# A hybrid decoder layer on one core: 1/rms goes into the matrix that x is turned with

## The chip, the cores and the metric

The kernel runs on one core of a Trainium2 chip, in one launch. The metric is the device time of an execution in microseconds; the median of three executions of the kernel before is 969.17 us (967.22 to 969.35). The page of the profile and the trace come from one further execution, recorded by the hardware profiler.

Engines are named as the profile names them: PE is TensorE's matrix products and PEld its weight loads, DVE is VectorE, ACT is ScalarE, POOL is GpSimd, SP is the engine whose queue issues most of the DMAs.

## The reference, cut to what matters

The layer normalises x over its 1024 features, modulates it with a vector that comes from the conditioning input c, and multiplies the result by one wide input matrix. Everything behind that (a gated convolution, a chunked retention in four heads, an output projection, a residual and a last norm) is untouched by the change.

```python
mod = silu(c) @ ada_w + ada_b
shift, scale, gate = split(mod, 3)
y = x * rsqrt(mean(x * x, axis=-1) + 1e-6)        # one factor for each of the 1024 positions
u = y * norm_g * (1 + scale) + shift              # one factor and one shift for each feature
proj = u @ w_in                                   # contracts over the features
```

The product with `w_in` contracts over the features, so u has to lie with its features on the partitions, while x comes from memory with its positions there. The factor 1/rms belongs to a position, the modulation to a feature.

## The kernel before, in words

All 1024 positions are kept on chip. x is read in eight tiles `xt` of 128 positions by 1024 features (line 170). The function `norm` (lines 172 to 188) handles one tile:

- ACT squares the tile and sums the squares into `ms` (line 175); POOL adds epsilon and raises it to the power -1/2 (lines 176, 177).
- DVE multiplies the whole tile by that factor, in place (line 178).
- PE turns the tile in two groups `xp` of four 128x128 blocks, by transposes against the identity `ident_t` (line 183). Each group is one PSUM bank, and four banks take turns.
- ACT copies the first group, DVE the second, into `xs`, which holds x turned (lines 186, 188); for the last tile DVE copies both.

Around it, `mod` (lines 190 to 200) makes the shift and the factor of one block of 128 features from a 1 MB tile `aw` of the modulation matrix: DVE does two dot products against the broadcast activation (line 193), except that the shift of block 0 is eight small products of PE (`mod0p`, line 197). `make_u` (lines 202 to 206) then makes u for that block and splits it into a rounded part `uh` (ACT) and the rest `ul` (DVE), because each product with a weight is done as three products of rounded operands (lines 82, 83, 84: uh with the weight's high part, ul with the high part, uh with the weight's low part). Block 0 is done in two halves of the positions, blocks 1 to 7 whole.

The first eight output tiles (the `ps_e` and `ps_p..` sums) accumulate over the eight feature blocks, 24 products of 512 columns for each block, while `aw` and the weights of the next blocks still arrive. This is the head of the kernel. `ps_s` follows (line 367), then 21 pairs of output tiles by a seven-product scheme (lines 469 to 493) with the convolution's taps on DVE beside them, then the retention in chunks interleaved with the values and the pointwise product (lines 540 to 703), then the output projection and the last norm. For the seven-product scheme DVE and ACT make sums of quarters of u, split as `th` and `tl` (lines 317 to 326); that work also starts in the head.

The order of every engine's instructions is set when the program is built: a list scheduler with a cost model of its own takes the code's dependences and priorities and writes one fixed order for each engine. DVE, ACT, POOL, SP and PE each run theirs strictly in order and wait by semaphores. So a changed cost in one place can move instructions elsewhere in the program. The buffers of `aw` are three, so the load for block 3 waits until block 0's `aw` has been read, by DVE and by `mod0p`.

Of the kernel before, what the change touches and what calls it, by code (L numbers as in the profile page):

```python
# [7 lines left out]
F32 = mybir.dt.float32  # L8
# [4 lines left out]
P = 128  # L13
# [34 lines left out]
def hybrid_layer(ctx: ExitStack, tc: tile.TileContext, x, vec, c_row, ada_ss, ada_g, adab_g, w_e, w_s, w_p, w_v,  # L48
                 w_pw, w_out, final_g, cs, masks, kc, ident, out):
    nc = tc.nc  # L50
    SUB, ADD, MUL = ALU.subtract, ALU.add, ALU.mult
# [47 lines left out]
    ident_t = const.tile([P, P], F32, name="ident_t")  # L99
# [36 lines left out]
    hp = head_ctx.enter_context(tc.tile_pool(name="head", bufs=1))  # L136
# [8 lines left out]
    def head():  # L145
# [26 lines left out]
        def norm(t, xt_):  # L172

            ms = hp.tile([P, 1], F32, tag="ms", name=f"ms{t}", bufs=3)
            nc.scalar.activation(junk2, xt_, AF.Square, scale=D ** -0.5, accum_out=ms)
            nc.gpsimd.tensor_scalar(ms, ms, EPS, None, op0=ADD)
            nc.gpsimd.tensor_tensor(ms, ms, mhalf[:, 0:1], op=ALU.pow)
            nc.vector.tensor_scalar(xt_, xt_, ms, None, op0=MUL)
            for q in range(2):
                tp = hps.tile([P, 4, P], F32, tag=("paa", "pbb", "pcc", "pdd")[(2 * t + q) % 4], name=f"xp{t}{q}")  # L180
                for j in range(4):
                    k = 4 * q + j
                    nc.tensor.transpose(tp[:, j], xt_[:, k * P:(k + 1) * P], ident_t)
                dst = xs[:, 4 * q:4 * q + 4, t * P:(t + 1) * P]
                if q == 0 and t < 7:
                    nc.scalar.copy(dst, tp)
                else:
                    nc.vector.tensor_copy(dst, tp)
# [36 lines left out]
        for t in range(4):  # L225
            norm(t, xts[t])
        mod(0, aw)
        make_u(0, halves(0))
        for t in range(4, TT):
            norm(t, xts[t])  # L230
# [520 lines left out]
    with tc.tile_pool(name="fin", bufs=1, reuse_waits="tile") as fp, \  # L751
# [92 lines left out]
        t = TT - 1  # L844
# [98 lines left out]
```

## Time and profile before

| | |
|---|---|
| median of three executions | 969.17 us (967.22 to 969.35) |
| the profiled execution | 970.08 us, of which 968.3 us are the span from the first to the last instruction |
| PE busy | 937.2 us, 97% of the span |
| DVE busy | 745.3 us, 77% |
| ACT busy | 412.2 us, 43% |
| POOL busy | 389.8 us, 40% |
| DMA | 154.95 MB, 160 GB/s in the mean |

Busy time is the time in which an engine had an instruction in it. The ends of PE's products are modelled, and products overlap: the time that one costs in a stream is the distance from one start to the next, which is shorter than the duration that a row gives. Where the text needs it, it is worked out from a row that covers several in a stream: (length of the row less the duration of one) divided by their count less one.

### The profile page before, as it was taken

What the parts mean: (1) busy time and instruction counts of PE and PEld (TensorE: products, weight loads), DVE (VectorE), ACT (ScalarE), POOL (GpSimd) and SP (SyncE); (2) the same over time, 40 slices, a digit from 0 to 9 for tenths busy, and PEclk for the clock granted to TensorE, in tenths of its full rate; (3) what the DMA queues carried; (4) which work ended last, traced back from release to release, by engine and by line L of the source; (5) the groups of instructions that cost most, each with busy time, mean ns of one, the idle gap of its engine ahead of it and who ended that gap; (6) DMA issues with size and microseconds to landing.
All of it is one profiled execution on the core that took longest, in us unless ns stands there. A gap on an engine that the chain in (4) does not pass through costs nothing.

```text
span 968.3 us, 12531 instructions
## 1 busy us (share of the span) xinstructions
PE 937.2 (97%) x4496; PEld 784.5 (81%) x4496; DVE 745.3 (77%) x928; ACT 412.2 (43%) x676; POOL 389.8 (40%) x358
## 2 busy tenths in 40 slices
PE   7999999999999999999999899989999999999996
PEld 5788888888888888888888688877788887888886
DVE  6999989899999999999799786687875344523322
ACT  7775433433434334343430575677634333311201
POOL 3004987877887798878550111121022100000000
PEclk9999999999999999999999899989999999999998
DMA  9924242333334444443434799555775486432111
GB/s 348 331 78 133 75 144 88 118 88 104 125 121 138 133 127 132 134 141 97 154 117 163 267 332 308 179 165 200 240 290 176 157 279 221 147 106 87 65 44 44
DMA packets 84673, 154.95 MB, mean 160 GB/s; under 512 B 6657, under 2 KB 43265, under 8 KB 83330
## 3 DMA queue, kind: packets, MB, share of 16 engines
q1 hardware_dynamic: 81986, 147.07, 45.9%
q0 software_dynamic: 1040, 3.67, 1.0%
q10 hardware_dynamic: 1584, 3.41, 0.9%
q8 instruction: 35, 0.57, 0.2%
q14 instruction: 28, 0.23, 0.1%
HBM read 107.99 MB, written 46.14 MB: 159 GB/s over the span
## 4 chain that ended last, share of the span: by engine, by line
PE 78%; DVE 10%; DMA 5%; issue 3%; ACT 2%; POOL 1%; POOLq 0%; DVEq 0%; ACTq 0%
PE pa L83 7%; PE pa L84 7%; PE pa L82 7%; DVE y L271 4%; PE ps_o L83 4%; PE ps_o L84 4%; PE ps_o L82 4%; PE pb L83 4%; PE pb L82 4%; PE pb L84 4%; PE ps_pw L82 2%; PE ps_pw L84 2%; PE ps_pw L83 2%; DMA wo<-w_out 2%; PE pd L84 2%
## 5 line engine op out<-in xcount | busy, mean ns | idle before, releaser
L271 DVE SCALAR_TENSOR_TENSOR yp<-a,vec_t,yp 128x1024 f32<-128x1024 f32 x210 | 269.7, 1284 | 6.7 <-ACT yp L269 2.7
L334 POOL TENSOR_TENSOR pl<-pr,ph 128x512 fp32r<-128x512 f32 x63 | 84.7, 1345 | 59.7 <-ACT ph L333 59.5
L334 POOL TENSOR_TENSOR pl_s<-sm_s,ph_s 128x512 fp32r<-128x512 f32 x63 | 85.4, 1356 | 36.6 <-ACT ph_s L333 35.1
L333 ACT CAST ph_s<-sm_s 128x512 fp32r<-128x512 f32 x63 | 39.1, 622 | 95.8 <-PE pa L83 80.3
L333 ACT CAST ph<-pr 128x512 fp32r<-128x512 f32 x63 | 39.1, 622 | 79.7 <-PE pa L83 45.4
L806 POOL TENSOR_TENSOR fr<-fr,mhalf 128x1 f32<-128x1 f32 x7 | 3.8, 547 | 168.0 <-DVE fr L805 168.0
L691 POOL TENSOR_TENSOR rs<-mv,kc_t 128x2 f32<-128x2 f32 x16 | 6.2, 390 | 158.7 <-DVE mv L688 133.8
L82 PE MATMUL pb<-uh,ph_s 128*128 128x512 f32 x168 | 65.4, 389 | 0.0
L84 PE MATMUL pb<-uh,pl_s 128*128 128x512 f32 x168 | 65.4, 389 | 0.0
L82 PE MATMUL pa<-th,ph_s 128*128 128x512 f32 x168 | 65.4, 389 | 0.0
L83 PE MATMUL pb<-ul,ph_s 128*128 128x512 f32 x168 | 65.4, 389 | 0.0
L84 PE MATMUL pa<-th,pl_s 128*128 128x512 f32 x168 | 65.4, 389 | 0.0
L83 PE MATMUL pa<-tl,ph_s 128*128 128x512 f32 x168 | 65.4, 389 | 0.0
L346 POOL TENSOR_TENSOR sm_s<-pr,pr 128x512 f32<-128x512 f32 x42 | 57.2, 1362 | 17.3 <-DMA pr<-w_p 10.1
L83 PE MATMUL ps_pw<-zl,hi_pw 128*128 128x512 f32 x128 | 50.4, 394 | 2.2 <-DVE zl L71 2.2
L84 PE MATMUL ps_pw<-zh,lo_pw 128*128 128x512 f32 x128 | 50.6, 395 | 0.0
L82 PE MATMUL ps_pw<-zh,hi_pw 128*128 128x512 f32 x128 | 48.0, 399 | 1.9 <-ACT zh L70 1.7
L271 DVE SCALAR_TENSOR_TENSOR y<-a,vec_t,y 128x1024 f32<-128x1024 f32 x30 | 44.1, 1469 | 6.9 <-ACT y L269 6.1
L797 DVE TENSOR_TENSOR g<-ps_o,gate 128x512 f32<-128x512 f32 x14 | 9.5, 691 | 49.7 <-PE ps_o L84 49.7
L83 PE MATMUL ps_o<-wol,hi_yc 128*128 128x512 f32 x112 | 43.8, 391 | 0.1
L83 PE MATMUL ps_o<-wol,hi_yr 128*128 128x512 f32 x112 | 43.7, 393 | 0.0
L84 PE MATMUL ps_o<-woh,lo_yc 128*128 128x512 f32 x112 | 43.6, 390 | 0.0
(447 smaller groups left out, 2792.9 us busy)
## 6 DMA issues: line engine op xcount, KB each, us to landing
pr<-w_p SPq DMA_DIRECT2D x84, 256.0 KB, 2.7
aw<-ada_ss SPq DMA_DIRECT2D x8, 1024.0 KB, 8.1
d_qk<-ro SPq DMA_DIRECT2D x16, 512.0 KB, 3.3
wo<-w_out SPq DMA_DIRECT2D x16, 512.0 KB, 4.7
xt<-x SPq DMA_DIRECT2D x8, 512.0 KB, 6.9
d_sg<-o SPq DMA_DIRECT2D x16, 256.0 KB, 2.6
sg<-d_sg SPq DMA_DIRECT2D x16, 256.0 KB, 3.5
v<-d_v SPq DMA_DIRECT2D x16, 256.0 KB, 3.4
```

What stands on the lines that cost most here:

```text
L82: nc.tensor.matmul(ps, lh, rh, start=start, stop=False, skip_group_check=more)
L83: nc.tensor.matmul(ps, lh, rl, start=False, stop=False, skip_group_check=more)
L84: nc.tensor.matmul(ps, ll, rh, start=False, stop=stop, skip_group_check=more)
L271: nc.vector.scalar_tensor_tensor(acc, ap[:, j:j + S], col(V_CW, m * CW + j), acc, op0=MUL, op1=ADD)
L333: nc.scalar.copy(hi, src)
L334: nc.gpsimd.tensor_tensor(lo, src, hi.bitcast(F32), op=SUB)
L346: nc.gpsimd.tensor_tensor(out, a, b, op=op)
L691: nc.gpsimd.tensor_tensor(rs, mv[:, :, 1], kc_t[:, K_G2 + 2 * h:K_G2 + 2 * h + 2], op=MUL)
L797: nc.vector.tensor_tensor(g[:, :n], ps(), gate[:, sl], op=MUL)
L806: nc.gpsimd.tensor_tensor(r, r, mhalf[:, 0:1], op=ALU.pow)
```

## The change

DVE no longer multiplies the tile. It multiplies the 128x128 identity by the factor 1/rms instead, one factor for each partition, which gives a diagonal matrix `dgx` (three buffers). PE does not transpose the scaled tile against the identity, but multiplies the unscaled blocks as they came by the diagonal matrix, as ordinary products of fp32: block^T times diag(1/rms) is the turned and scaled block. What is added up and where it is copied to stays as it was.

```diff
@@ -175,12 +175,13 @@
             nc.scalar.activation(junk2, xt_, AF.Square, scale=D ** -0.5, accum_out=ms)
             nc.gpsimd.tensor_scalar(ms, ms, EPS, None, op0=ADD)
             nc.gpsimd.tensor_tensor(ms, ms, mhalf[:, 0:1], op=ALU.pow)
-            nc.vector.tensor_scalar(xt_, xt_, ms, None, op0=MUL)
+            dg = hp.tile([P, P], F32, tag="dg", name=f"dgx{t}", bufs=3)
+            nc.vector.tensor_scalar(dg, ident_t, ms, None, op0=MUL)
             for q in range(2):
                 tp = hps.tile([P, 4, P], F32, tag=("paa", "pbb", "pcc", "pdd")[(2 * t + q) % 4], name=f"xp{t}{q}")
                 for j in range(4):
                     k = 4 * q + j
-                    nc.tensor.transpose(tp[:, j], xt_[:, k * P:(k + 1) * P], ident_t)
+                    nc.tensor.matmul(tp[:, j], xt_[:, k * P:(k + 1) * P], dg, start=True, stop=True)
                 dst = xs[:, 4 * q:4 * q + 4, t * P:(t + 1) * P]
                 if q == 0 and t < 7:
                     nc.scalar.copy(dst, tp)
```

Every line of the program behind line 178 moves down by one. The built order changes too, in three places that matter here.

On PE, at the end of the turning of x, this stood before (`xp60` is tile 6, first group; a row with x4 is four instructions):

```order
L183 MATMUL xp60_287<-ident_t_76,xt6_92 128x128 x4
L183 MATMUL xp61_293<-ident_t_76,xt6_92 128x128 x4
L197 MATMUL mod0p_234<-cact_82,aw0_148 128x1 x8
L183 MATMUL xp70_304<-ident_t_76,xt7_93 128x128 x4
L183 MATMUL xp71_310<-ident_t_76,xt7_93 128x128 x4
L82 MATMUL ps_e00_319<-uh0_94,weh0_152 128x512
```

And this stands there now:

```order
L184 MATMUL xp60_294<-dgx6_292,xt6_92 128x128 x3
L198 MATMUL mod0p_238<-cact_82,aw0_148 128x1 x8
L184 MATMUL xp60_294<-dgx6_292,xt6_92 128x128
L184 MATMUL xp61_300<-dgx6_292,xt6_92 128x128 x4
L184 MATMUL xp70_312<-dgx7_310,xt7_93 128x128 x4
L184 MATMUL xp71_318<-dgx7_310,xt7_93 128x128 x4
L82 MATMUL ps_e00_327<-uh0_94,weh0_152 128x512
```

The eight products of `mod0p` now have 51 of the 64 blocks of x ahead of them, where they had 56.

On DVE, from the copy of the last group of x to the first `ul` of block 1, this stood before from `ul0` on:

```order
L206 TENSOR_TENSOR ul0_102<-xs_123,uh0_94 128x512
L193 SCALAR_TENSOR_TENSOR junk_132,mod1_359<-aw1_351,cbc_130 128x1024
L206 TENSOR_TENSOR ul0_102<-xs_123,uh0_94 128x512
L320 TENSOR_TENSOR xs_123<-xs_123 128x512
L166 TENSOR_TENSOR wel1_356<-wer1_353,weh1_355 128x512
L193 SCALAR_TENSOR_TENSOR junk_132,mod2_399<-aw2_391,cbc_130 128x1024 x2
L206 TENSOR_TENSOR ul1_103<-xs_123,uh1_95 128x1024
```

And this stands there now, from that copy on:

```order
L189 COPY xs_123<-xp71_318 128x4x128
L207 TENSOR_TENSOR ul0_102<-xs_123,uh0_94 128x512
L194 SCALAR_TENSOR_TENSOR junk_132,mod2_407<-aw2_399,cbc_130 128x1024
L207 TENSOR_TENSOR ul0_102<-xs_123,uh0_94 128x512
L321 TENSOR_TENSOR xs_123<-xs_123 128x512
L194 SCALAR_TENSOR_TENSOR junk_132,mod2_407<-aw2_399,cbc_130 128x1024
L207 TENSOR_TENSOR ul1_103<-xs_123,uh1_95 128x1024
```

Both dot products of block 1 and the split of its weight went ahead of the copy of the last group; behind it six instructions stand up to and with `ul1`.

On DVE, at the end of the head, between `ul` of block 6 and of block 7, this stood before:

```order
L206 TENSOR_TENSOR ul6_108<-xs_123,uh6_100 128x1024
L321 TENSOR_TENSOR xs_123<-xs_123 128x512
L166 TENSOR_TENSOR wel7_596<-wer7_593,weh7_595 128x512
L71 TENSOR_TENSOR tl2_673<-xs_123,th2_670 128x512
L322 TENSOR_TENSOR xs_123<-xs_123 128x512
L206 TENSOR_TENSOR ul7_109<-xs_123,uh7_101 128x1024
```

And this stands there now:

```order
L207 TENSOR_TENSOR ul6_108<-xs_123,uh6_100 128x1024
L322 TENSOR_TENSOR xs_123<-xs_123 128x512
L324 TENSOR_TENSOR xs_123<-xs_123 128x512
L166 TENSOR_TENSOR wel7_604<-wer7_601,weh7_603 128x512
L323 TENSOR_TENSOR xs_123<-xs_123 128x512
L71 TENSOR_TENSOR tl2_681<-xs_123,th2_678 128x512
L71 TENSOR_TENSOR tl3_682<-xs_123,th3_679 128x512
L71 TENSOR_TENSOR tl4_683<-xs_123,th4_680 128x512
L324 TENSOR_TENSOR xs_123<-xs_123 128x512
L71 TENSOR_TENSOR tl2_681<-xs_123,th2_678 128x512
L71 TENSOR_TENSOR tl3_682<-xs_123,th3_679 128x512 x2
L207 TENSOR_TENSOR ul7_109<-xs_123,uh7_101 128x1024
```

Eleven instructions now lie between the two, where there were four.

## Rows read from the trace of the kernel before

**Rows 1.** The page: busy us by engine, share of the span, instructions.

```profile
PE 937.2 (97%) x4496; PEld 784.5 (81%) x4496; DVE 745.3 (77%) x928; ACT 412.2 (43%) x676; POOL 389.8 (40%) x358
```

**Rows 2.** Stretches: from:to, length, busy of PE, PEld, DVE, ACT, POOL, granted clock, DMA.

```profile
22.50:69.00 46.50, 44.61 (x193) 35.96 (x194) 46.47 (x71) 37.23 (x55) 0.00 (x0) 1.00 0.60 208
69.00:536.00 467.00, 465.55 (x2053) 385.06 (x2051) 445.24 (x431) 178.47 (x298) 340.74 (x257) 1.00 0.39 124
536.00:780.00 244.00, 230.33 (x1334) 201.31 (x1335) 171.49 (x318) 139.85 (x233) 36.26 (x71) 0.97 0.68 234
```

**Rows 3.** Waits of PE, 23 to 69 us: total us, times, longest us.

```profile
PE ps_e L83 <- DVE ul L206: 1.3, 3, 0.7
PE ps_e L82 <- ACT uh L204: 0.7, 1, 0.7
```

**Rows 4.** Timeline, 0 to 45 us: start, length, engine, instruction, count, idle before.

```profile
7.90 0.75 DVE L178 TENSOR_SCALAR xt<-xt,ms 128x1024 f32<-128x1024 f32 x1 [0.25 <-POOL ms L177]
...
15.69 1.06 PE L183 MATMUL xp<-ident_t,xt 128*128 128x128 f32 x8 [0.66 <-DVE xt L178]
...
19.50 1.87 PEld L197 LDWEIGHTS mod0p<-cact,aw 128*128 128x128 f32 x16
...
21.89 0.33 SPq L157 DMA_DIRECT2D aw<-ada_ss  x1
...
23.14 0.73 PE L82 MATMUL ps_e<-uh,weh 128*128 128x512 f32 x2 [0.75 <-ACT uh L204]
```

**Rows 5.** Lines by form: the multiplication removed; count, busy us, mean ns, idle before.

```profile
L178 DVE TENSOR_SCALAR xt<-xt,ms 128x1024 f32<-128x1024 f32 x8 | 6.0, 750 | 0.8 <-POOL ms L177 0.7
```

**Rows 6.** Line 583, which scales the identity in the convolution's norm: min/median/max ns.

```profile
L583 DVE TENSOR_SCALAR rs_d<-ident_t,rstd x8: 273/281/286, 634.6 to 641.3; 128x128 f32<-128x128 f32 x8
```

**Rows 7.** Timeline of PE, 3 to 12 us.

```profile
3.42 3.78 PE L221 MATMUL cp<-crow,ones_t 1*128 1x512 f32 x4 [3.42 <-ACT crow L210]
8.71 3.68 PE L183 MATMUL xp<-ident_t,xt 128*128 128x128 f32 x16 [1.51 <-DVE xt L178]
```

**Rows 8.** Timeline near 639 us: four products of fp32 with a diagonal matrix, 128 columns.

```profile
638.85 1.11 PE L584 MATMUL rb<-rs_d,ones_t 128*128 128x128 f32 x8
```

**Rows 9.** The tile xp in the windows 13.2 to 13.7 and 14.2 to 14.8 us.

```profile
L183 PE MATMUL xp<-ident_t,xt x4: 421/421/422, 12.9 to 13.5; 128*128 128x128 f32 x4
...
L183 PE MATMUL xp<-ident_t,xt x8: 272/273/324, 13.9 to 14.8; 128*128 128x128 f32 x8
```

**Rows 10.** Lines by form, 0 to 80 us: ACT's instructions in the head.

```profile
L175 ACT ACTIVATE junk<-xt 128x1024 bf16<-128x1024 f32 x8 | 8.5, 1062 | 3.3 <-DMA xt<-x 3.3
...
L165 ACT CAST weh<-wer 128x512 fp32r<-128x512 f32 x8 | 4.9, 614 | 2.2 <-PE ps_pdd L83 2.2
...
L186 ACT COPY xs<-xp 128x512 f32<-128x512 f32 x7 | 4.1, 579 | 1.0 <-PE xp L183 0.9
...
L200 ACT ACTIVATE gsc<-mod,scg,vec_t 128x1 f32<-128x1 f32 x8 | 3.1, 386 | 6.4 <-DVE junk L193 6.3
...
L204 ACT ACTIVATE uh<-xs,shift,gsc 128x512 fp32r<-128x512 f32 x2 | 1.6, 814 | 0.0
```

**Rows 11.** Timelines of DVE and of PE near 62 us: ul of block 7.

```profile
61.43 0.69 DVE L322 TENSOR_TENSOR xs<-xs 128x512 f32<-128x512 f32 x1
62.03 1.22 DVE L206 TENSOR_TENSOR ul<-xs,uh 128x1024 fp32r<-128x1024 f32 x1
...
65.35 0.39 PE L83 MATMUL ps_e<-ul,weh 128*128 128x512 f32 x1
```

**Rows 12.** The chain that ended last, near 32 us: start, length, what.

```profile
31.92 0.50 PE ps_e L83
```

**Rows 13.** The page: loads of the modulation matrix, KB each, us to landing.

```profile
aw<-ada_ss SPq DMA_DIRECT2D x8, 1024.0 KB, 8.1
```

**Rows 14.** Stretches in the retention, columns as in rows 2.

```profile
543.00:550.00 7.00, 6.01 (x28) 6.04 (x29) 6.94 (x11) 5.48 (x8) 0.00 (x0) 0.51 0.87 313
...
628.50:638.50 10.00, 7.78 (x33) 7.20 (x34) 7.84 (x21) 5.42 (x12) 3.25 (x5) 0.50 0.68 232
```

## The prediction

> **What bounds the kernel now.** I read the page first, then the sums by stretch, then PE's waits, and only then the stretch that is changed. The page shows PE busy for 97% of the span [rows 1]; the sums by stretch show where the rest lies. From 69 to 536 us PE is busy for 465.55 of 467 us, so nothing of VectorE shows there, and a shift at 69 us passes through unchanged; the retention from 536 to 780 us has most of the idle time, 244.00 - 230.33 = 13.7 us [rows 2]. In the head (22.5 to 69 us) VectorE is busy without a break, 46.47 of 46.50 us [rows 2], which looks as if it were the limit, but PE's waits in that stretch are only 1.3 us for VectorE's `ul` and 0.7 us for ACT's `uh` [rows 3]. PE and VectorE are nearly level there. So what counts is when PE can start the head's products, 23.14 us before [rows 4], and how much it waits behind that.
>
> **What the change removes.** Eight multiplications of 750 ns on VectorE [rows 5], against eight of the 128x128 form, which take 281 ns where the kernel already scales its identity [rows 6]: 8 x 0.47 = 3.8 us less of VectorE. For the first tile that lies on the path: VectorE's instruction starts at 7.90 us, when POOL's factor is there [rows 4], and PE at 8.71 [rows 7]. PE can start at 8.71 - 0.47 = 8.24 us. The other seven are beside PE's work and count only if VectorE is the limit, which is weighed below.
>
> **What it adds on PE.** A transpose is one pass. A product of two fp32 operands is two: `mod0p` is eight products in the program and 16 weight loads in the trace [rows 4], and the four products of line 584's inner loop are eight records [rows 8]. In a stream at the full clock, where one takes 0.27 us from start to end [rows 9], a transpose costs (1.06 - 0.27)/7 = 0.112 us [rows 4]; a pass of line 584 costs (1.11 - 0.27)/7 = 0.12 us with a slow first one in it [rows 8], and one of `mod0p` at most 1.87/16 = 0.117 us [rows 4]. I take 0.112 for a pass too, so a block costs 0.223 us in place of 0.112. At the lower clock, in which PE begins, transposes come every (3.68 - 0.42)/15 = 0.217 us [rows 7]. Two passes of 128 columns at that clock are not shown; the nearest rows are two transposes, 0.43 us, and the 512-column passes of line 221, at most 3.78/4 = 0.95 us each, so 0.47 us for two of a quarter of the width [rows 7]. I take 0.43.
>
> When the clock rises is a choice. The transposes take 421 ns up to 13.5 us and 273 ns from about 14 us [rows 9], that is 1.2 and 2.4 GHz, after PE had transposed without a real pause since 8.71. I keep 14.0 us, since PE is as dense as before from 8.24 us on.
>
> The Trainium skill has a rule that speaks against the products altogether: its page "TensorE: Matmul & The Clock Gate", section "Terms", says that the transpose mode is four times faster for FP32. By it a block would cost 0.45 us at the full clock; line 584's row shows two passes of the usual length, so the trace does not agree, and I go by the row. As a case of its own it stands among the rivals.
>
> **The sum up to the first product of the head.** From 8.24 to 14.0 us, 5.76/0.43 = 13.4 blocks. The other 50.6 cost 50.6 x 0.223 = 11.3 us, and `mod0p` stands among them with 16 x 0.112 = 1.8 us: 14.0 + 13.1 = 27.1 us. Before, PE waited between tiles for VectorE and ACT; now it is the slowest of the chain. ACT's square and copy of a tile, 1.06 + 0.58 us [rows 10], fit into the 8 x 0.223 = 1.8 us that a tile takes PE, and VectorE's part is smaller still. What stood between the last transpose and the head, ACT's `uh` of block 0, is now early: `mod0p` has 51 blocks ahead of it, ends at 14.0 + 37.6 x 0.223 + 1.8 = 24.2 us, and ACT needs its shift (under 0.39) and one `uh` of 0.81 us [rows 10], so 25.4 us. PE runs on without a wait at 27.1 us, 4.0 us later than 23.14.
>
> **What is given back, and what is added, up to 69 us.** VectorE now does both dot products of block 1 before the last copy of x, so only six instructions lie between that copy and the end of `ul1`: by the starts one of 512 columns takes 0.60 us; one of 1024 takes 1.22, or 1.14 with the same overlap [rows 11]. The copy can start at 27.1 + 0.3 us; it, three of 512 and three of 1024 columns give 27.4 + 0.6 + 1.8 + 3.4 = 33.2 us. Before, PE took `ul1` at 31.9 us, after a wait [rows 12]. VectorE is 1.3 us later, PE 4.0: the three waits for `ul` go, 1.3 us [rows 3], and with each the slow first product, 0.50 - 0.39 = 0.11 us [rows 11, 12], in all 1.6 us. This is all that VectorE's 3.8 us can give PE here.
>
> Two waits come in their place. First, ACT has eight instructions from the end of `mod0p` (24.2 us, plus 0.3 for the last one's length) to the second half of `uh0`: 0.81 x 3 + 0.61 + 0.58 + 0.39 x 3 at most [rows 10] = 4.8 us, so 28.5 to 29.3 us with starts that overlap or not. PE, after four products of the first half at 44.61/193 = 0.23 us [rows 2], wants it at 28.0. I take 0.6 us (0 to 1.2). Second, `ul7`. It was ready at 62.03 + 1.22 = 63.25 us and used at 65.35, 2.1 us of slack [rows 11]. Seven more instructions of 0.60 us now stand ahead of it, 4.2 us, and VectorE is 1.3 us later: 68.8 us. PE wants it at 65.35 + 4.0 - 1.6 + 0.6 = 68.35. I take 0.4 us (0 to 2).
>
> The loads do not decide. The load of `aw` for block 3 was issued at 21.89 us on SP's queue [rows 4]; now it waits for `mod0p`'s reading, 24.2 us, and stands behind the load of block 2's weight there, 0.3 us. With 8.1 us to land [rows 13] it is there at 32.6 us, and VectorE first reads it behind `ul1`, at 33.2 us; PE uses what comes of it only after all of block 2, so that a later landing has that much cover still.
>
> Sum at 69 us: +4.0 - 1.6 + 0.6 + 0.4 = **+3.4 us**. Bounds: with the clock up only at 17.5 us it is 9.26/0.43 = 21.5 blocks, 42.5 x 0.223 = 9.5 and 1.8, so 28.8 us, and with both new waits at their upper ends 5.7 - 1.6 + 3.2 = +7.3; with the clock up at 11.1 us (the first rival) and no new wait 2.6 - 1.6 = +1.0.
>
> **Behind 69 us.** Up to 536 us PE has no idle time that could take the shift up [rows 2]. In the retention the built order interleaves the chunks, the values and the pointwise products differently, and 13.7 us of PE's idle time lie there. Nothing in the trace prices an order that was not run. I take 0, with a quarter of that idle time, 3.4 us, either way.
>
> The profiled execution took 970.08 us (span 968.3 and 1.8 us around it), 0.9 above the median of the runs. So the forecast is 973.5 us against that execution, and 969.2 + 3.4 = **972.6 us** against the median.
>
> **Rivals.**
>
> *The clock rises earlier.* Products of PE proper might raise it sooner than transposes did. For it: PE has only a short pause before 8.24 us. Against: the products of line 221 kept PE busy for 3.78 us from 3.42 [rows 7], and the transposes behind them still ran at the lower clock. If it rose at 11.1 us, half-way: 2.9/0.43 = 6.7 blocks before, 57.3 x 0.223 = 12.8 behind, and 1.8: 25.7 us, a shift of 2.6, and with -0.6 as above +2.0: 971.2 us. The Trainium skill, page "TensorE: Matmul & The Clock Gate", section "Part 4: PE-mode transpose", gives a reason for this one: the full clock does not engage for transposes, since they do not count as busy as products do. The trace disagrees in that nothing but transposes ran when it rose near 14 us [rows 9]. Chance 0.17.
>
> *A block costs four passes.* 0.86 us at the lower clock, 0.45 at the full one: 6.7 blocks to 14.0 us, 57.3 x 0.45 = 25.8, and 1.8: 41.6 us, a shift of 18.5; VectorE's waits would all vanish, -1.6: about 986 us. Against it stand the counts of records [rows 4, 8]. Chance 0.03.
>
> *The retention takes it back.* The idle time there falls by 2 to 4 us in the new order: 969 to 971 us, no change. Chance 0.15.
>
> *Faster.* The place is the retention: from 543 to 550 and from 628.5 to 638.5 us the granted clock is 0.5 [rows 14], with PE busy for 6.01 of 7 and 7.78 of 10 us. If the new order closes the waits that led there, these busy times fall to half, by 6.9 us, and 973.5 - 6.9 - 0.9 = 965.7 us. It decides only if both stretches go, since one alone (3 to 3.9 us) just pays for the head. Against it: nothing of the change touches what PE waits for there. Chance 0.08.
>
> *VectorE is the limit of the head*, so that its 3.8 us come straight off. For it: 46.47 of 46.50 us busy. Against: PE waits for it 1.3 us in all, so that it can give no more than that. It is in the sum.
>
> **How the numbers follow.** The forecast has 0.57, the clock 0.17, the retention as no change 0.15, faster 0.08, four passes 0.03. The time is that of the forecast. The range is 968.8 to 976.5 us: 3.4 us of the retention on either side, with the early clock and the upper ends of the two waits. A measurement of this kernel can tell about 0.2%, 1.9 us, from no change, so no change is 967.2 to 971.1 us. Half of the early clock falls in there, and with the retention's case it is 0.23: faster 0.08, no change 0.23, slower 0.57 + 0.09 + 0.03 = 0.69.
>
> **What would show it.** Right: PE's blocks of x as 128 records in place of 64, without idle time between tiles, at twice the distance; the first product of the head near 27 us with no wait; waits for `ul` below 0.5 us up to 60 us, one for `uh0` near 28 us and a small one for `ul7` near 68 us; `ps_s` about 3.4 us later than before; VectorE's multiplications at 0.28 us. Wrong: the first product of the head before 25 us (the clock, or cheaper passes) or behind 29; a wait for `aw` in the head; or the sum of PE's idle time from 536 to 780 us off 13.7 by more than 3.4 us, in which case the order there, not the change of arithmetic, sets the sign.

## The result, and the profile after

The changed kernel takes **978.64 us** in the median of four runs (975.26 to 979.43), the kernel before beside it 969.26 (967.22 to 971.46): a ratio of **1.0084** [1.0064, 1.0103], slower with an interval well clear of no change. The forecast was 972.6 us, with 976.5 as its upper end. The sign was right, the size was not: of the 9.4 us between the medians the prediction found 3.4.

The profiled execution after took 975.26 us, the shortest of the four. Read stage by stage, its own 975.26 - 970.08 = 5.2 us over the profiled execution of before do not lie where the prediction put them. The page, against [rows 1], and then the stretches, against [rows 2], with the last one new:

```profile
PE 944.0 (97%) x4560; PEld 789.3 (81%) x4560; DVE 739.8 (76%) x928; ACT 410.8 (42%) x676; POOL 388.3 (40%) x358
```

```profile
22.50:69.00 46.50, 45.21 (x214) 37.37 (x214) 46.34 (x71) 35.46 (x54) 0.00 (x0) 1.00 0.57 207
69.00:536.00 467.00, 466.79 (x2060) 386.29 (x2059) 442.54 (x431) 180.58 (x301) 339.31 (x257) 1.00 0.38 122
536.00:780.00 244.00, 231.26 (x1342) 201.13 (x1341) 170.84 (x318) 137.50 (x232) 37.77 (x71) 0.97 0.68 232
785.00:945.00 160.00, 156.41 (x677) 125.79 (x676) 60.07 (x70) 36.35 (x52) 3.29 (x6) 1.00 0.41 132
```

PE has 4560 records for 4496, the 64 second passes, and VectorE 5.5 us less of work. From 785 to 945 us PE is now busy for 156.41 of 160 us. The same stretch of the kernel before:

```profile
785.00:945.00 160.00, 159.79 (x700) 130.86 (x698) 59.98 (x71) 36.52 (x54) 3.83 (x7) 1.00 0.40 130
```

This is the output projection, of which the prediction says nothing. PE's waits in it were none and are now these (the second row; the first is the head, against [rows 3]):

```profile
PE ps_e L83 <- DVE ul L207: 1.2, 1, 1.2
...
PE ps_o L82 <- ACT woh L70: 3.3, 4, 1.3
```

The head first, in PE's timeline (start, length, count; lines behind 178 are one higher than before), to be held against [rows 4, 7]:

```profile
7.99 13.40 PE L184 MATMUL xp<-dgx,xt 128*128 128x128 f32 x102 [0.84 <-DVE dgx L179]
21.23 1.84 PE L198 MATMUL mod0p<-cact,aw 128*128 128x1 f32 x16
22.93 3.15 PE L184 MATMUL xp<-dgx,xt 128*128 128x128 f32 x26
25.83 0.71 PE L82 MATMUL ps_e<-uh,weh 128*128 128x512 f32 x2
```

The 128 passes run without a pause, and `ps_e` follows at 25.83 us, 2.7 us later than before. The clock rose earlier than forecast, as the passes of `xp` in two windows show (the 421 ns ones against the 275 ns ones, as in [rows 9]):

```profile
L184 PE MATMUL xp<-dgx,xt x5: 421/421/421, 10.3 to 11.1; 128*128 128x128 f32 x5
...
L184 PE MATMUL xp<-dgx,xt x8: 274/275/275, 11.7 to 12.5; 128*128 128x128 f32 x8
```

Where the projection loses its time stands in SP's queue. After:

```profile
764.34 0.32 SPq L734 DMA_DIRECT2D cgl<-d_cg  x1
772.93 0.32 SPq L738 DMA_DIRECT2D d_yc<-cgl  x1
773.30 1.25 SPq L760 DMA_DIRECT2D wo<-w_out  x2
```

and before:

```profile
764.67 0.32 SPq L733 DMA_DIRECT2D cgl<-d_cg  x1
765.04 0.90 SPq L759 DMA_DIRECT2D wo<-w_out  x2
765.99 0.42 SPq L770 DMA_DIRECT2D fgt<-final_g  x1
773.43 0.33 SPq L737 DMA_DIRECT2D d_yc<-cgl  x1
```

A store of `d_yc` that waits for VectorE's product until 772.9 us now stands ahead of the first two of sixteen loads of `w_out`. They are issued at 773.30 in place of 765.04 us. All sixteen pass through two buffers, so each waits for the splitting of the last but one, and the chain of what ended last runs through them:

```profile
783.81 3.45 DMA d_yc<-cgl
...
788.33 2.91 SPq L791
...
791.35 6.08 DMA wo<-w_out
797.45 1.05 ACT woh L70
798.53 1.24 DVE wol L71
799.78 4.99 DMA wo<-w_out
```

I use two measures below. The head ends with the last product of `ps_e`: 67.3 us before, 69.7 after. *Behind the head* is a kernel's median less that time of its profile: 969.2 - 67.3 = 901.9 us before, 978.6 - 69.7 = 908.9 after. Most of the loss, about 7 us, is behind the head. The median is of several executions and the head of one, so a single value is good to a microsecond or two: by the two profiled executions alone, spans less heads, it is 901.0 and 903.7 us.

### The profile page after: what moved, and what is told of

Read it like the earlier page. It is cut to its first block, busy times and chain, and to the rows that moved or that the text cites. A ratio compares the mean times of both kernels' runs of the same rounds, so it can differ in the third digit from the quotient of the medians.

```text
span 973.4 us, 12654 instructions
## 1 busy us (share of the span) xinstructions
PE 944.0 (97%) x4560; PEld 789.3 (81%) x4560; DVE 739.8 (76%) x928; ACT 410.8 (42%) x676; POOL 388.3 (40%) x358
## 4 chain that ended last, share of the span: by engine, by line
PE 76%; DVE 10%; DMA 6%; ACT 3%; issue 2%; POOL 1%; SPq 0%; POOLq 0%; ACTq 0%; DVEq 0%
PE pa L82 7%; PE pa L84 7%; PE pa L83 7%; DVE y L272 4%; PE ps_o L83 4%; PE ps_o L84 4%; PE ps_o L82 4%; PE pb L84 3%; PE pb L82 3%; PE pb L83 3%; DMA wo<-w_out 3%; PE ps_pw L82 2%; PE ps_pw L83 2%; PE ps_pw L84 2%; PE pd L84 2%
## 5 line engine op out<-in xcount | busy, mean ns | idle before, releaser
L335 POOL TENSOR_TENSOR pl_s<-sm_s,ph_s 128x512 fp32r<-128x512 f32 x63 | 84.9, 1347 | 35.3 <-ACT ph_s L334 22.3
```

What stands on the lines that cost most here:

```text
L335: nc.gpsimd.tensor_tensor(lo, src, hi.bitcast(F32), op=SUB)
```

## Experiments

Two theories at the start. *H*: the second passes make the whole rise, through the head. *O*: the head costs what it shows and the rest is the new order of instructions. The first results brought up a third, *F*: PE's own code. The experiments exchange or move instructions in the finished program, behind the scheduler, so that the order of every queue is known.

### Arithmetic and order apart: b_full, a_old, b_prod, a_move

```diff
 # b_full: the program of before, each instruction in its place
-TENSOR_SCALAR xt <- xt, ms                TENSOR_SCALAR of 128x1024
+TENSOR_SCALAR dg[t] <- ident_t, ms        of 128x128
-MATMUL xp <- ident_t, xt   is_transpose=True
+MATMUL xp <- dg[t], xt     is_transpose=None
 #         (the eight blocks of dg lie in a tile enlarged for them)
 # a_old: the same exchange backwards, in the program of the changed kernel
 # b_prod: before, with is_transpose=None alone
 # a_move: the changed kernel; SP's store d_yc<-cgl6 from ahead of wo8 to behind fgt
```

> The whole change (diagonal built by VectorE, 64 products of two passes) in the instruction order of the kernel before: the order of every queue is that of before, only the 8 multiplications and the 64 transposes are exchanged. Nothing of the computation is left out. Theory O (most of the 9.4 us between the medians is the new order, above all the store of d_yc by SyncE ahead of the first two loads of w_out): the head's +2.4 us at 69 us stays, the projection's +5.1 us is gone, so 971.7 us (970.5 to 973.5). Theory H (the products themselves make the whole rise, through the head and through what it delays): 978.6 us as the changed kernel, not under 976.

> The arithmetic of the kernel before (VectorE scales x, one-pass transposes against the identity) in the instruction order of the changed kernel. Nothing is left out. Theory O: the head is that of before, the projection keeps its late weights, 969.3 + 5.1 = 974.4 us (973 to 976.5), and PE waits 5 to 10 us in all for woh in the projection. Theory H: 969.3 us (within 1 us), no waits for woh.

> The changed kernel with one instruction moved: SyncE's store of d_yc from cgl6 stands behind the loads wo8, wo9 and fgt as in the kernel before, instead of ahead of wo8. Theory O: wo8 is issued at about 767 us instead of 773.3, the waits of PE for woh go, 978.6 - 5.1 = 973.5 us (972 to 975). A weaker form of O (the loads of raw_yc and h1 ahead of wo13 are the cause, not this store): 978 us. Theory H: 978.6 us.

> The kernel before, in its own order, with the 64 transposes made plain products with the identity (two passes instead of one); VectorE's multiplication stays. Nothing is left out. Theory O: what the second pass costs in the head alone, first ps_e at 26 to 27 us instead of 23.1, 971.5 to 973 us. Theory H: 978 us. If b_full is under this by 0.3 to 0.7 us, the earlier start that the diagonal gives is real in the end time.

Measured, against 969.62 us of before on that chip: b_full 977.09 (1.0081 [1.0057, 1.0105]), a_old 978.06 (1.0092 [1.0070, 1.0114]), a_move 978.14 (1.0082 [1.0060, 1.0105]), b_prod 978.20 (1.0085 [1.0065, 1.0105]).

No theory foresaw this: the arithmetic alone costs 7.5 to 8.6 us, the order alone 8.4, both together 9.4. H, whose numbers fit b_full and b_prod, falls with a_old, which has no second pass. O falls with b_prod, which has the order of before. The head of b_prod ends at 71.9 us, +4.6; so 4.0 us more are lost behind it, in an unchanged order. What b_prod and b_full share beside the head is longer code: the built program of PE has 578,944 bytes before and in a_old, 587,136 in b_prod, b_full and the changed kernel. The page has a DMA queue for code, and its size is that of PE's program (578,944 bytes are 35.3 blocks of 16 KB). Before and after:

```profile
q8 instruction: 35, 0.57, 0.2%
```

```profile
q8 instruction: 36, 0.59, 0.2%
```

35 fetches make 0.57 MB, so one brings 16 KB, and 8,192 bytes more near the start move all later ones by half a block against the work. At one place the trace shows one of them among the data. In 5.5 us near 650 us, at the same place of the work, the kernel before and b_prod have (packets, MB, share; below, us from issue to landing):

```profile
q1 hardware_dynamic: 821, 0.79, 48.1%
...
k<-d_qk SPq DMA_DIRECT2D x1, 256.0 KB, 3.3
d_yr<-sg SPq DMA_DIRECT2D x1, 256.0 KB, 3.5
q<-d_qk SPq DMA_DIRECT2D x1, 256.0 KB, 3.8
```

```profile
q1 hardware_dynamic: 802, 0.77, 43.8%
q8 instruction: 1, 0.02, 1.2%
...
k<-d_qk SPq DMA_DIRECT2D x1, 256.0 KB, 5.0
d_yr<-sg SPq DMA_DIRECT2D x1, 256.0 KB, 5.1
q<-d_qk SPq DMA_DIRECT2D x1, 256.0 KB, 5.0
```

With the fetch among them the three take 1.2 to 1.7 us longer, and ACT stands idle for `k`, where before it did not (what of this reaches PE is not shown):

```profile
656.28 0.62 ACT L70 CAST kch<-k 128x512 fp32r<-128x512 f32 x1 [1.72 <-DMA k<-d_qk]
```

### Is it the code? b_nop128, bp_nop128, b_nop64; and the store alone, b_move

```diff
 # ahead of the first MATMUL of PE's program, 128 times (64 in b_nop64):
+EVENT_SEMAPHORE   PE waits for DVE >= 1, which is met
 # b_move: before; SP's store d_yc<-cgl6 from behind fgt to ahead of wo8
```

> The kernel before with 128 more instructions at the start of PE's program (semaphore waits that are already met, no work, while PE waits for crow). They make PE's program 8,192 bytes longer, as the 64 second passes do (578,944 to 587,136 bytes). Nothing of the computation changes. Theory F (PE's code is fetched in blocks of 16 KB by queue 8; half a block more code shifts every fetch against the work, and the fetches then fall on the transfers of the retention): the fetches lie at about 45, 70, 102 us ... as in b_prod, and the time rises by the 3 to 4 us that b_prod lost behind 69 us: 973 us (971.5 to 975). Theory O or a plain shift of the work: 969.6 us, within 0.8.

> b_prod (before's order, products of two passes with the identity) with the same 128 instructions at PE's start: the second passes and they make together one whole block of 16 KB, so that the fetches stand against the work as in the kernel before. Theory F: the head keeps its +4.5 us and nothing is lost behind it, 969.6 + 4.5 = 974.1 us (973 to 975.5). Rival (the loss behind the head comes from the head's delay itself): 978.2 us as b_prod, or more by what the 128 instructions take.

> As b_nop128, with 64 instructions: PE's program is 4,096 bytes longer, a quarter of a block. Theory F gives no sign for a quarter; it expects a time that differs from 969.6 us by 1 us or more in either direction, with the differences in the retention (540 to 785 us). Rival: 969.6 us, within 0.8.

> The kernel before with one instruction moved: SyncE's store of d_yc from cgl6 stands ahead of the load wo8, as in the changed kernel, instead of behind wo9 and fgt. Theory O: wo8 is issued at about 773 us instead of 765.0, PE waits for woh in the projection, 969.6 + 5.1 = 974.7 us (973 to 976). Rival (the loads of raw_yc and h1 ahead of wo13 are the cause): 969.6 us within 1.

Measured, against 969.39 us: b_nop128 984.08 (1.0149 [1.0136, 1.0162]), bp_nop128 983.51 (1.0138 [1.0123, 1.0153]), b_nop64 973.38 (1.0042 [1.0025, 1.0059]), b_move 975.17 (1.0053 [1.0040, 1.0066]).

The met waits were not free: 128 of them held `cp` back to 14.96 us, and all totals expected were too low by that. So the head is taken off. b_nop128's ends at 77.1 us and leaves 907.0 behind it, 5 us more than before; bp_nop128's ends at 80.9, later still, and leaves 902.6. The half block costs, and a second half block gives it back, although it delays the head by another 3.8 us. The rival, that the head's delay does it, is out. The fetches stand where theory F has them (starts in the trace's DMA records, less the end of the head, us):

```
before      546 571 593 618 643 661 682
bp_nop128   546 570 592 618 642 660 682     + 16 KB
b_prod      556 582 605 633 658 675 696     + 8 KB
b_nop128    556 583 609 633 658 675 697     + 8 KB
```

b_move shows the other cause by itself, in the order and with the code of before: 5.8 us for one store moved. PE's waits from 780 us on:

```profile
PE ps_o L82 <- ACT woh L70: 4.3, 3, 1.7
PE ps_o L83 <- DVE wol L71: 0.7, 1, 0.7
```

### The same with products: b_warm32, b_warm64, a_warm32, bf_warm32

```diff
 # ahead of the first MATMUL, 32 times (64 in b_warm64); one is two weight loads and two passes:
+MATMUL cp0[:, 0:1] <- ones_t[0:1, 0:1], ones_t[0:1, :]    128x1, overwritten by cp
 # a_warm32: in the changed kernel; bf_warm32: in b_full
```

> The kernel before with 32 small products (128 ones against a single one, into the accumulator that cp overwrites) at the start of PE's program, where PE waits for crow until 3.4 us. They make PE's program 8,192 bytes longer, half a block of its code fetches, as the changed kernel's second passes do, and may let the clock rise before 14.0 us. Nothing of the computation changes. Theory F: behind 69 us 4 to 5 us are lost as in b_nop128, whatever the head does: with a head changed by -2 to +2 us, 971.5 to 976.5 us. Rival (only delays of the head cost something behind it): 969.4 us plus the head's change.

> The same with 64 small products: 16,384 bytes more, one whole block, so that the fetches stand against the work as in the kernel before. Theory F: nothing is lost behind 69 us; with a head changed by -2 to +4 us (if the 64 take over 3.4 us they push cp), 967.4 to 973.4 us, and behind the head 3 us or more less than b_warm32. Rival: behind the head as b_warm32, within 1 us.

> The changed kernel with 32 such products at PE's start: with its second passes (half a block) they make a whole block. Theory F, if it holds under the changed order too: 978.6 less about 4 behind the head, and the head changed by -3 to +1 us: 971.5 to 975.5 us. Theory O alone (the loss is in the order of the projection): what the head gains, 975.5 to 979.5 us.

> The whole change in the order of the kernel before (as b_full) with 32 such products at PE's start: a whole block more code than the kernel before. Theory F: the head's +4.5 us less what an earlier clock gives, and nothing lost behind it: 971 to 974 us, 3 to 4 us under b_full's 977.1 plus the head's difference. If the clock is at full speed by 9 us, the blocks' two passes cost 0.223 us instead of 0.43 from the start and the head is within 2 us of before's. Rival: 977 us plus the head's change.

Measured, against 968.55 us: b_warm32 982.63 (1.0144 [1.0117, 1.0170]), b_warm64 991.67 (1.0252 [1.0222, 1.0282]), a_warm32 987.91 (1.0200 [1.0173, 1.0227]), bf_warm32 983.39 (1.0147 [1.0119, 1.0176]).

As clock-warmers they failed: they delayed the head by 9.4 (32) and 23.3 us (64) and raised no clock (last section). As code they did what F says: 905.9 us behind the head with half a block, 901.0 and 902.0 with a whole one. Under the changed order a_warm32 keeps 906.6, 2.3 under the changed kernel but 4.7 over before.

### What is left of the changed kernel: a_fix, a_fixw, b_nop192, b_wide

```diff
 # a_fix: the changed kernel, SP's queue (a_fixw: and 32 products of ones as above)
-cgl7, d_yc6, wo8, wo9, fgt, h10, wo10, wo11, d_yc7, wo12, raw_yc0, raw_yc1, h11, wo13, wo14, raw_yr2, raw_yc2, wo15
+cgl7, wo8, wo9, fgt, d_yc6, h10, wo10, wo11, d_yc7, wo12, wo13, raw_yc0, raw_yc1, wo14, h11, wo15, raw_yr2, raw_yc2
 # b_nop192: 192 met waits, as b_nop128
 # b_wide: before, with a product of ones 128x512 ahead of cp and one of 128x256 ahead of xp
```

> The changed kernel with SyncE's order at the start of the projection put as in the kernel before: the store of d_yc from cgl6 behind fgt, wo13 ahead of raw_yc0 and raw_yc1, wo14 ahead of h11, wo15 ahead of raw_yr2 and raw_yc2. Its half block of PE code stays. If order and fetches are separate: behind the head 905 to 906 us as b_prod and b_full (the changed kernel 908.9), so 978.6 - 3 = 975.5 us (974 to 977), PE waits under 2 us for woh. If the order of the loads does not matter by itself: 978.6 us.

> a_fix with the 32 small products at PE's start (a whole block more code than the kernel before; the head ends at about 81.3 us as in a_warm32). If order and fetches together make up the loss: behind the head 902 us as in the kernel before, 983.3 us (982 to 985), 4 to 5 us under a_warm32's 987.9. If something else is lost in the changed order: 986 to 988 us.

> The kernel before with 192 met waits at PE's start, three quarters of a block more code; the head ends at about 67.3 + 192 x 0.106 - 3.4 = 84.3 us. Behind the head the kernel before has 901.9 us, a quarter of a block 903.3, half a block 906.0. Theory F expects between 900 and 905 us behind it, by where the fetches fall; if the loss were only the head's delay or a matter of odd code, it would be 906 us as with half a block.

> The kernel before with two wide products of ones in PE's idle time at the start, one of 512 columns before cp (into the tile that cp overwrites) and one of 256 columns between cp and the first xp. If the clock rises earlier by the 2 us that real products start earlier, the head gains up to 1.2 us: 968.0 us (967 to 969.4). If the head is set by VectorE and the loads of x anyway: 969.4 us. PE's program grows by 512 bytes, which moves the fetches by 1 us.

Measured, against 969.15 us: a_fix 979.83 (1.0099 [1.0079, 1.0119]), a_fixw 987.85 (1.0190 [1.0171, 1.0210]), b_nop192 985.71 (1.0169 [1.0145, 1.0193]), b_wide 968.98 (0.9994 [0.9980, 1.0008]).

a_fix is a miss, though SP's queue in it is not yet that of before (d_yc7 still stands ahead of wo12, and h10 ahead of wo10): the last load of `w_out` is issued 43.5 us behind the first product of `ps_o`, where before it is 37.2 and in the changed kernel 42.3. Three quarters of a block (b_nop192) leave 901.8 us behind the head, as none. a_fixw has 906.3 us behind the head, about as much as a_warm32 without the moves (906.6). b_wide's head ends 0.7 us earlier and its time can't be told from before's: it is the only kernel here as fast as the one before, and none is faster.

### The store that a_fix missed: a_fix2, a_fix2w

```diff
 # a_fix2: a_fix, and SP's store d_yc<-cgl7 (a_fix2w: and 32 products of ones)
-... wo11, d_yc7, wo12, wo13 ...
+... wo11, wo12, d_yc7, wo13 ...
```

> a_fix with one more move: the store of d_yc from cgl7 behind wo12, so that SyncE's queue from cgl7 to wo2 is that of the kernel before. If the queue order is the cause: the last load of w_out is issued at +37 to +39 us after the first ps_o, PE waits for woh under 2 us, the projection takes 156 to 158 us as in b_full instead of 160.8, and behind the head 905 to 906 us: 975.5 us (974 to 977.5). If the order of the other engines (VectorE's splits, PE's products) sets the supply: the last load at +42 us or later and 978 to 980 us.

> a_fix2 with 32 small products at PE's start (a whole block more code than the kernel before; head until about 81.4 us). If queue order and fetches are all: behind the head 902 us, 983.4 us (982 to 985). If the order of the other engines counts: 986 to 988 us as a_warm32 and a_fixw.

Measured, against 969.51 us: a_fix2 980.80 (1.0118 [1.0102, 1.0135]), a_fix2w 986.90 (1.0180 [1.0162, 1.0197]). A miss again: the last load is issued at +43.1 us, as the alternative in the expectation has it, though 980.80 us is 0.8 above its range. But SP's queue is still not quite that of before, as the expectation takes it to be: the load of `h10` stands ahead of wo10 and wo11, where before it stood behind both. It waits until the store at 776.84 has landed, and they wait with it:

```profile
776.84 0.33 SPq L738 DMA_DIRECT2D d_yc<-cgl  x1
779.46 0.33 SPq L791 DMA_DIRECT2D h<-x  x1
779.88 9.29 SPq L760 DMA_DIRECT2D wo<-w_out  x3
```

VectorE, in its changed order, multiplies `cgl` of the last block first and splits wo10 after it, so that the third load in that row, which needs wo10's buffer, is held until 789 us:

```profile
786.32 1.37 DVE L737 TENSOR_TENSOR cgl<-ps_pw,cgl 128x512 f32<-128x512 f32 x2 [7.24 <-PE ps_pw L84]
787.61 1.22 DVE L71 TENSOR_TENSOR wol<-wo,woh 128x1024 fp32r<-128x1024 f32 x1
```

In the kernel before the split comes first, while PE still works on that block:

```profile
780.53 1.23 DVE L71 TENSOR_TENSOR wol<-wo,woh 128x1024 fp32r<-128x1024 f32 x1 [4.86 <-ACT woh L70]
782.91 1.37 DVE L736 TENSOR_TENSOR cgl<-ps_pw,cgl 128x512 f32<-128x512 f32 x2 [1.15 <-PE ps_pw L84]
```

So VectorE's order is enough to hold that load, wherever `h10` stands. What SP's whole queue of before would give back under the changed order of the other engines was not run.

### All runs in one table

Code is what PE's program has more than before. The medians are from several chips, on which the kernel before took 968.6 to 969.6 us. The last two columns are from the profiles: from the first `ps_pw` to the first `ps_o`, and from there to the last `ps_o`. They hold what the clock did in that one execution too: in the `ps_pw` stage PE ran at a granted clock of 0.5 for 10.2 us in b_full, for 3.4 in b_prod, b_nop128, b_warm32, bp_nop128 and bf_warm32, and not at all in before.

```
            order    code KB  head ends  median  behind it   pw stage  projection
before      before     0        67.3     969.2     901.9      133.2      155.2
b_wide      before     0.5      66.6     969.0     902.4      133.5      154.5
b_nop64     before     4        70.1     973.4     903.3      133.5      156.5
b_prod      before     8        71.9     978.2     906.3      136.5      156.5
b_full      before     8        71.8     977.1     905.3      139.1      156.5
b_nop128    before     8        77.1     984.1     907.0      136.5      155.8
b_warm32    before     8        76.7     982.6     905.9      135.5      156.3
b_nop192    before    12        83.9     985.7     901.8      135.3      155.1
bp_nop128   before    16        80.9     983.5     902.6      134.1      155.2
bf_warm32   before    16        81.4     983.4     902.0      136.1      155.7
b_warm64    before    16        90.7     991.7     901.0      133.5      154.6
b_move      1 store    0        67.1     975.2     908.1      132.5      161.0
after       changed    8        69.7     978.6     908.9      133.3      160.8
a_move      changed    8        71.0     978.1     907.2      138.6      158.4
a_fix       changed    8        71.3     979.8     908.5      133.1      161.7
a_fix2      changed    8        69.5     980.8     911.3      136.3      161.5
a_old       changed    0        69.0     978.1     909.0      136.8      162.4
a_warm32    changed   16        81.3     987.9     906.6      135.3      160.3
a_fixw      changed   16        81.6     987.9     906.3      136.8      160.1
a_fix2w     changed   16        80.2     986.9     906.7      135.0      160.2
```

In the order of before, the four kernels with half a block more have 905.3 to 907.0 us behind the head, before and the three with a whole block 901.0 to 902.6: 906.1 against 901.9 in the mean, **4.2 us**, whatever made the code longer and however late the head was. The granted clock explains little of it: a fit of all runs, with one level for each kernel and one slope for a run's mean granted clock (0.5 us for 0.001), leaves 3.3 us at equal clock. A quarter of a block has 903.3, three quarters 901.8; why these cost so little, F does not say. In the changed order, half a block has 907.2 to 911.3 (mean 909.0), a whole one 906.3 to 906.7 (mean 906.5): 2.5 us. But a_old, which has no code added, stands at 909.0 too, so that the half block is not shown to cost anything there.

The three transfers of above, of `k`, `d_yr` and `q`, can be looked up in all twelve profiles with the order of before. In the four with half a block a fetch falls among them, and they take 12.0 to 15.1 us added up; in the other eight none does, and they take 10.3 to 10.6.

## Why the prediction was wrong, point by point

**What VectorE is spared: right.** `dgx` takes 281 ns a tile, as expected, and PE starts at 7.99 us (forecast 8.24).

**A block costs two passes: right.** 128 records, (13.40 - 0.28)/101 = 0.130 us apart over both clocks, (3.15 - 0.28)/25 = 0.115 at the full one. With it the rival of four passes is out. The rule behind it, from the Trainium skill's page "TensorE: Matmul & The Clock Gate", section "Terms", that transposes are four times faster for FP32, does not hold here: the product has two passes of the length of the transpose's one.

**When the clock rises: a matter of the execution.** In the profile of the changed kernel it was at 11.7 us, and the first product of `ps_e` at 25.83, the early-clock rival (25.7). In a_move, whose head is the same program, it rose at 14.2 us, and the product came at 27.07, the forecast (27.1). The rival, with a chance of 0.17, came true in two of the four profiles of this head (after and a_fix2). The four end it at 69.5 to 71.3 us, +3.1 in the mean, against a forecast of +3.4. So this term of the sum holds.

**The waits for `ul` vanish, -1.6: right in the changed order only.** There one wait is left, 1.2 us for `ul7`, forecast at 0.4; the one for `uh0`, forecast at 0.6, did not come. From its first to its last product the head takes 43.9 us in all four profiles, 0.3 less than before; the forecast was 0.6 less. In the order of before the waits stay, as b_full's from 20 to 74 us show,

```profile
PE ps_e L83 <- DVE ul L207: 1.7, 3, 0.7
```

and b_full's head takes 44.7 us and ends at +4.5. The new order is worth 0.8 us to the head.

**Up to 536 us unchanged: right**, 466.79 of 467 us. PE's idle time from 536 to 780 us is 244.00 - 231.26 = 12.7 us in this profile, 1 us less than before, well within the 3.4 us allowed for it.

**"Behind 69 us ... I take 0": the step that failed.** It looked for what a new order could do only in PE's idle time, found that in the retention, and put no term on the projection, since PE does not wait there before. Measured is +6.3 us behind the head (978.6 less 70.4, the mean head of these four kernels, against 901.9). Two causes were missed.

- *The order of the projection.* a_old has only the order of the changed kernel, and 909.0 - 901.9 = 7.1 us more behind the head; its projection takes 162.4 us in place of 155.2. With a whole block of code, so with the fetches in place, the changed order has 906.5 - 901.9 = 4.6 us more, and the projection takes 160 us. That one store in SP's queue can do it is shown by b_move (+5.8 us). That it alone did it in the changed kernel is refuted: a_move, a_fix and a_fix2 put SP's queue back bit by bit, all but the load of `h10`, and gained nothing that can be told from noise. VectorE's order and the load of `h10` hold the same chain of sixteen loads.
- *Half a block of code*, 4.2 us in the order of before. No step of the prediction asked where PE's code comes from. In the changed order its share is between nothing (against a_old) and 2.5 us (against a whole block).

So 3.1 of the 9.4 us lie in the head, nearly as forecast, and 6.3 behind it; the changed order alone (a_old) is enough for those, and how they divide between order and code is not shown. That the sign was right is in part luck: the head's term gave it, but two thirds of the rise came from a place that had none.

What stays open: why a_old, with before's arithmetic and code in the changed order, has 909.0 us behind the head where the whole-block kernels of that order have 906.5 (its head ends +1.7 us though its transposes are those of before, with one new wait of 2.4 us for `xs`); and by which of PE's waits the shifted fetches cost their 4 us. The transfers near 651 us are slower in all four half-block kernels in the order of before, but no wait of PE was followed back to them. Their stage from `ps_pw` to `ps_o` is longer too (135.5 to 139.1 us, against 133.2 before), but bf_warm32 and b_nop192, which lost nothing, have 136.1 and 135.3 there. The retention's half-speed stretches, too, differ from profile to profile: one of 6.8 us, some 475 us behind the head, is in all, the later ones vary in number and length with the same program order, so that theory of a gain by the order there was neither shown nor excluded.

The range failed for the same reason as the sum: it held the retention's 3.4 us and the head's waits, and nothing for a stage in which PE never waited. Its upper end is also lower than its own terms added up: 972.6 + 3.4, with the two waits 2.2 us above their middle, is 978.2 us and not 976.5, still short of 978.64.

## What to carry to other kernels

A stage in which the bounding engine never waits can still be at its edge: before a reordering is called neutral, follow its supply (here sixteen loads through two buffers behind one queue) and ask how many us of lead the first load has. Compare the built order of every queue over the whole program, the DMA queues first, not only at the changed lines. When a change alters the number of instructions of the busiest engine early in the program, test it beside versions padded with idle instructions, and take off what those cost themselves: a few us can belong to the code's place and not to the edit.

## What the runs showed of the hardware that was not expected

**PE's code is part of the DMA traffic.** One fetch of 16 KB comes every 18 to 27 us in the retention (the fence of starts above), and its place against the data is worth 4.2 us of 970 in the order of before (3.3 at equal granted clock). The Trainium skill's page "Runtime: NRT & Kernel Launch", section "Instruction fetch mechanics", has the blocks of 16 KB too, and calls what they cost mostly hidden. The sizes agree; the cost measured here does not, if the whole program's time is counted.

**A met wait on PE is not free.** 64, 128 and 192 of them ahead of `cp` put its start at 8.05, 14.96 and 21.85 us: 6.9 us for 64, so 0.108 us each. The first rows of b_nop128 and of b_nop192:

```profile
14.96 3.74 PE L221 MATMUL cp<-crow,ones_t 1*128 1x512 f32 x4 [14.96 <-issue]
```

```profile
21.85 3.75 PE L221 MATMUL cp<-crow,ones_t 1*128 1x512 f32 x4 [21.85 <-issue]
```

**Products of one column cost as much as wide ones, and the clock was low behind 27 us of them.** In b_warm64:

```profile
1.05 27.46 PE L221 MATMUL cp<-ones_t 1*128 1x1 f32 x128 [1.05 <-DVE mhalf L104]
28.38 3.76 PE L221 MATMUL cp<-crow,ones_t 1*128 1x512 f32 x4
32.07 6.45 PE L183 MATMUL xp<-ident_t,xt 128*128 128x128 f32 x32
```

A pass of one column costs 27.46/128 = 0.215 us, as much as one of 128 columns at 1.2 GHz [rows 7]. PE had an instruction in it from 1.05 us on, and yet the transposes at 32.07 us began at the low clock: 32 in 6.45 us are 0.2 us each, against 0.112 at 2.4 GHz. It rose at 37.7 us.
